# Hybrid block, start of the first projection: features 0 to 255 of x are multiplied without their shift, which is added later as a bias; x is scaled on VectorE and GpSimd

## The chip, the core and the metric

The kernel runs on one core of a Trainium2 chip. The metric is the device time of one execution in microseconds; the median of three runs is given. A core has TensorE (PE, with its weight loads as PEld), VectorE (DVE), ScalarE (ACT), GpSimd (POOL) and SyncE (SP). Here SP issues the DMAs. Each engine has its own queue of instructions and works through it in order; semaphores order the engines among each other.

## What is computed

One transformer block on x of 1024 tokens by 1024 features, in float32. Of the reference only the first part matters here:

```
cond = jax.nn.silu(c)
mod = cond @ w_ada[l] + b_ada[l]
sh_a, sc_a, gt_a, sh_m, sc_m, gt_m = jnp.split(mod, N_MOD, axis=-1)
h = rms_norm(x, g_attn_pre[l]) * (1 + sc_a) + sh_a
proj = h @ w_in[l]
```

The projection is followed by rotary embedding, two kinds of attention, an output projection, a residual add, and an MLP with a squared ReLU (1024 to 4096 and back). w_ada is 1024 by 6144; its columns 0 to 1023 give the shift sh_a and columns 1024 to 2047 the scale sc_a.

## The kernel before

**Order of the work.** The instructions are put in order by a list scheduler in the kernel's own Python code (`Sched`, L178). Each step has a modelled duration, dependencies, resources that it takes and gives back (buffers, PSUM banks), and a priority. `pick` (L263) takes for each engine the step that can start first; the key is start time, then priority, then order of creation (`PW`, L151, is 0). A step can have alternatives on several engines; then the one that would end first is taken, with 1.5 us in favour of POOL (`BONUS`, L149). The order that comes out is fixed in the program; on the chip each engine follows it and waits where it must.

**Precision.** Products are made at float32 accuracy from two parts: a value is split into a rounded high part (hi) and the rest (lo), and each dense product is three matmuls, hi·hi, lo·hi and hi·lo (L920, L921, L923).

**First stage.** The eight blocks of 128 tokens of x are loaded (L533), squared and summed on ACT (L629), their reciprocal root is taken on POOL (L468, L470), the block is scaled on ACT or DVE (L634, L635), transposed on PE (L642) and copied from PSUM by ACT or DVE (L646) into xnT, which has features on the partitions: 8 chunks k of 128 features by 1024 tokens.

**Modulation.** w_ada's 2048 columns come in four groups g of 256 features. A group is four tiles of 512 KB (L521), each with the shift's and the scale's 256 columns for two of eight row blocks. DVE multiplies the columns by cond and adds them up (L664, L666: eight instructions of 128x512 a group); PE sums over the partitions with a column of ones (L675), DVE makes from it the gain g_a and the shift s_a (L681 to L683). Group g covers the chunks k = 2g and 2g + 1. For each chunk `mod_chunk` (L693) makes the hi part on ACT (L705), the full value over it in xnT on ACT (L702) and the lo part on DVE (L708). Chunks 0 and 1 are done in two halves of 512 tokens, the others in one piece of 1024.

**First unit.** w_in's columns are used in six units of 384. The first unit's products run chunk by chunk as the chunks become ready (`first_unit`, L942), into six PSUM accumulators: halves x = 0 and 1 of the tokens, three column blocks c. 24 products an accumulator, 144 in all. The order is: chunks 0 and 1 for x = 0, then for x = 1, then chunks 2 and 3, 4 and 5, and at the end 6 and 7, an accumulator at a time. While PE waits early on, `filler` (L930) lets it multiply a tile of ones (L937) into the bank of the fourth accumulator, until that one is used itself. At the end `evac` (L794) takes an accumulator out of PSUM: rotary embedding on DVE, splitting into hi and lo, DMAs into the tiles of attention.

**Weights.** w_in's tiles come in through a ring of WS = 2 raw tiles, are rounded on ACT (L550), and the rest is taken on DVE (L555; for later units on DVE or POOL). `order0` (L482) is the order of the first loads on SP; the loads are issued in that order (`in_turn`, L501), each when its buffer is free.

**After the first unit** the other five units' projections (`proj_tile`, L974) stand beside the attention on PE; `prefer` (L2217) takes a dense product first while the projections lead the attention by less than LEAD = 0.8 of a unit. Output projection and MLP follow.

Of the kernel before, what the change touches and what calls it, by code (L numbers as in the profile page):

```python
# [177 lines left out]
class Sched:  # L178
# [57 lines left out]
    def spare(self, o):  # L236

        return self.slack if 15 <= o.prio < 25 else 2.5 if o.kind == "w" else 0.0
# [119 lines left out]
def hybrid_block(ctx: ExitStack, tc: tile.TileContext, x, positions, w_ada, b_ada, g_attn_post, w_in, w_out,  # L358
# [33 lines left out]
    WR, WS, NP, NV, NK, NQ, NT, NO = 6, 2, 4, 3, 2, 2, 2, 2  # L392
# [154 lines left out]
    def split_w(*a):  # L547
# [10 lines left out]
        if a[0] == 0:  # L558
            w_e[a] = op("DVE", t_dv(512), lo(V), [e], gives=[(r_wst, 1)], prio=3)
# [23 lines left out]
    e = op("ACT", 0.1, lambda: A.activation(cond[:], c_raw, AF.Exp, scale=-1.0), [e_c], prio=0)  # L583
# [6 lines left out]
    warm = p0.tile([P, KC], F32, name="warm")  # L590
# [35 lines left out]
    def x_block(tb):  # L626
        def f_sq():
# [5 lines left out]
        e = op(("ACT", "DVE"), (t_sb(D) + AP_COST, t_d2(D) + AP_DV),  # L633
               (lambda: A.mul(x_t[tb][:], x_t[tb][:], rstd[:, tb:tb + 1]),  # L634
                lambda: V.tensor_scalar(x_t[tb][:], x_t[tb][:], rstd[:, tb:tb + 1], None, ALU.mult)), [e], prio=2)  # L635
# [16 lines left out]

    def mod_group(g):

        b = {}
# [30 lines left out]
        for half in ((0, 1) if g == 0 else (None,)):  # L686
# [6 lines left out]
    def mod_chunk(k, eg, half):  # L693
# [6 lines left out]
        def full(eng):  # L700
            if eng is A:
                return lambda: A.activation(h, h, AF.Identity, bias=s_a[:, k:k + 1], scale=g_a[:, k:k + 1])  # L702
            return lambda: V.tensor_scalar(h, h, g_a[:, k:k + 1], s_a[:, k:k + 1], ALU.mult, ALU.add)

        eh = op("ACT", t_sb(n) + 2 * AP_COST, lambda: A.activation(hh, h, AF.Identity, bias=s_a[:, k:k + 1],  # L705
                                                                  scale=g_a[:, k:k + 1]), deps, prio=0)
        e = op("ACT", t_sb(n) + 2 * AP_COST, full(A), [eh], prio=0)
# [21 lines left out]
    e_turned = op("POOL", 1.8, f_turned, [e_rope] + e_rs, prio=0)  # L729
# [7 lines left out]
    def tables_a():  # L737
        e_tab0 = op("POOL", 1.9, lambda: init_tabs(slice(0, 1024)), [e_c, e_turned], prio=0)
# [203 lines left out]
    def first_unit():  # L942
# [6 lines left out]
        for i, (k, part, x, c) in enumerate(order):  # L949
# [10 lines left out]
            def after(k=k, part=part):  # L960
                if part:
                    tick()
                if k == KC - 1:
                    sc.filler = None
            d = dense(0.454 if part == 0 else 0.227, emit,
                      [w_e[0, w_at(0, c, k)[0]], (e_hl if part else e_hh)[k, x]] + (e_xn[0] + e_xn[1] if a == 5 else []),
                      takes=[(r, 1)] if first else [], after=after, gives=[(r_w, 1)] if last[w_at(0, c, k)[0]] == i else [])
            if k == KC - 1 and part:
                yield (0, x, c, lambda a=a: accs[a], d, r)

    for a in first_unit():
        evac(*a)

    def proj_tile(u, x, c):  # L974
        b = []
        for k in range(KC):
# [9 lines left out]
            d = dense(0.681, emit, [w_e[u, w_at(u, c, k)[0]]], takes=[(r_pj, 1)] if k == 0 else [], gives=gives, after=tick)  # L986
# [28 lines left out]
    def open_attention():  # L1015
        if any(x.t is None for x in e_tab[0] + e_tab[1] + list(e_hl.values())):
# [1198 lines left out]
    LEAD = 0.8  # L2215
# [27 lines left out]
```

## Time and profile before

| | us |
|---|---|
| median of three runs | 1117.04 |
| lowest and highest | 1116.61, 1117.36 |
| the profiled execution | 1117.15 |
| its span, first to last instruction | 1114.9 |
| busy in the span: PE, DVE, ACT, POOL | 1100.7, 819.5, 630.3, 247.9 |

The granted clock of TensorE is 1.00 throughout the stretches shown below. A profile comes from one execution, and its span leaves out what lies before the first and behind the last instruction. A matmul's end is modelled and matmuls overlap, so that the pitch of their starts tells more than their durations. A row of the timeline gives start, duration, engine, line, operation, output and inputs, shapes and count, and in brackets the idle time before it and what ended it. A row of a group gives busy time, mean duration in ns, and idle time before its instructions.

### The profile page before, as it was taken

How to read it: one execution, taken by the hardware profiler on the slowest of the kernel's cores; microseconds unless marked ns; L12 is line 12 of the kernel's file. 1: busy time of each engine (PE TensorE's matmuls, PEld its weight loads, DVE VectorE, ACT ScalarE, POOL GpSimd, SP SyncE). 2: the span in 40 equal slices, each digit the busy share in tenths (PEclk: the TensorE clock that was granted, in tenths of full speed). 3: DMA queues.
4: the chain of work that ended last, by engine and by line, in shares of the span. 5: the costliest groups of instructions: out<-in, count | busy, mean ns of one | idle time of the engine just before them, and what ended most of it. 6: DMA issues, size and time to landing. Idle time of an engine off the chain costs nothing.

```text
span 1114.9 us, 15568 instructions
## 1 busy us (share of the span) xinstructions
PE 1100.7 (99%) x5393; PEld 917.0 (82%) x5393; DVE 819.5 (74%) x1388; ACT 630.3 (57%) x1092; POOL 247.9 (22%) x316
## 2 busy tenths in 40 slices
PE   8999999999999999999999999999999999999996
PEld 7788888888888888888888888888888888888885
DVE  7877777666777666689798654798643996537998
ACT  8768776464656666577674335643154632347542
POOL 2158768666742231110000000000000000000003
PEclk9999999999999999999999999999999999999999
DMA  9756676454513734656751369521578013584104
GB/s 350 227 180 192 195 261 198 146 207 159 186 43 140 263 103 131 227 211 243 276 217 38 109 240 334 175 76 39 201 267 308 26 57 113 189 320 152 39 20 151
DMA packets 94110, 195.39 MB, mean 175 GB/s; under 512 B 9008, under 2 KB 31664, under 8 KB 94032
## 3 DMA queue, kind: packets, MB, share of 16 engines
q1 hardware_dynamic: 94032, 194.40, 50.3%
q8 instruction: 43, 0.70, 0.3%
q14 instruction: 35, 0.29, 0.1%
HBM read 141.80 MB, written 33.03 MB: 157 GB/s over the span
## 4 chain that ended last, share of the span: by engine, by line
PE 85%; DVE 7%; DMA 3%; issue 2%; ACT 1%; SPq 0%; POOL 0%; POOLq 0%; DVEq 0%; ACTq 0%
PE mlp_ps L2057 17%; PE mlp_ps L2055 17%; PE mlp_ps L2056 17%; PE pj L920 5%; PE pj L923 5%; PE pj L921 4%; PE s_ps L1203 3%; PE y_ps L1609 2%; PE y_ps L1611 2%; PE y_ps L1610 2%; PE o_ps L1338 2%; DMA wa<-in_w_ada 2%; PE pt_ps L1308 1%; PE s_ps L1258 1%; PE o_ps L1350 1%
## 5 line engine op out<-in xcount | busy, mean ns | idle before, releaser
L2055 PE MATMUL mlp_ps<-hw 128*128 128x512 f32 x896 | 348.9, 389 | 0.2 <-DVE u L2092 0.2
L2057 PE MATMUL mlp_ps<-hw 128*128 128x512 f32 x896 | 348.6, 389 | 0.0
L2056 PE MATMUL mlp_ps<-hw 128*128 128x512 f32 x896 | 348.6, 389 | 0.0
L2055 PEld LDWEIGHTS mlp_ps<-hw 128*128 128x128 f32 x896 | 168.2, 188 | 35.5 <-DVE u L2092 0.6
L2056 PEld LDWEIGHTS mlp_ps<-hw 128*128 128x128 f32 x896 | 168.2, 188 | 35.1
L2057 PEld LDWEIGHTS mlp_ps<-hw 128*128 128x128 f32 x896 | 168.2, 188 | 34.7
L1819 DVE TENSOR_TENSOR hw<-w,hw 128x1024 fp32r<-128x1024 f32 x96 | 114.6, 1221 | 98.1 <-ACT hw L1812 97.9
L1812 ACT CAST hw<-w 128x1024 fp32r<-128x1024 f32 x96 | 97.7, 1048 | 127.5 <-PE mlp_ps L2057 86.8
L2165 POOL TENSOR_TENSOR st<-st,nhalf 128x1 f32<-128x1 f32 x8 | 8.0, 1010 | 591.8 <-DVE st L2163 591.8
L920 PE MATMUL pj<-hw,w_hl 128*128 128x512 f32 x240 | 102.3, 426 | 0.0
L923 PE MATMUL pj<-hw,w_hl 128*128 128x512 f32 x240 | 94.6, 394 | 0.0
L921 PE MATMUL pj<-hw,w_hl 128*128 128x512 f32 x240 | 94.3, 393 | 0.0
L1326 DVE TENSOR_TENSOR ph<-pt_ps,ph 128x512 fp32r<-128x512 f32 (+1 forms) x110 | 69.1, 647 | 31.4 <-ACT ph L1322 31.0
L1812 ACT CAST hw<-u 128x1024 fp32r<-128x1024 f32 x48 | 48.6, 1051 | 63.2 <-PE mlp_ps L2057 63.2
L1322 ACT CAST ph<-pt_ps 128x512 fp32r<-128x512 f32 (+1 forms) x110 | 58.4, 556 | 31.5 <-PE pt_ps L1311 25.2
L1819 DVE TENSOR_TENSOR hw<-u,hw 128x1024 fp32r<-128x1024 f32 x48 | 56.9, 1218 | 17.8 <-ACT hw L1812 17.8
L1229 ACT ACTIVATE p_sb<-p_sb,mn 128x128 f32<-128x128 f32 (+3 forms) x64 | 49.7, 777 | 33.6 <-DVE mn L1222 32.9
L1234 POOL TENSOR_SCALAR p_sb<-p_sb,den 128x128 f32<-128x128 f32 (+3 forms) x64 | 49.8, 783 | 75.6 <-DVE den L1232 69.6
L2113 DVE TENSOR_TENSOR yacc<-yacc,mlp_ps 128x512 f32<-128x512 f32 x96 | 62.0, 681 | 3.3 <-PE mlp_ps L2057 3.3
L1070 POOL TENSOR_TENSOR ada_acc<-ada_acc,wa_st 128x512 f32<-128x512 f32 x42 | 55.6, 1323 | 3.5
L923 PEld LDWEIGHTS pj<-hw,w_hl 128*128 128x128 f32 x240 | 45.1, 188 | 10.4
L1609 PE MATMUL y_ps<-hw,oh 128*128 128x512 f32 x128 | 52.1, 407 | 0.0
(215 smaller groups left out, 1971.0 us busy)
## 6 DMA issues: line engine op xcount, KB each, us to landing
hw<-s_dram SPq DMA_DIRECT2D x84, 512.0 KB, 4.3
wa_st<-in_w_ada SPq DMA_DIRECT2D x32, 512.0 KB, 5.2
w<-in_w_up SPq DMA_DIRECT2D x32, 512.0 KB, 5.6
w<-in_w_down SPq DMA_DIRECT2D x32, 512.0 KB, 6.7
s_dram<-hw SPq DMA_DIRECT2D x28, 512.0 KB, 3.8
qt<-hl SPq DMA_DIRECT2D x40, 256.0 KB, 2.6
w_st<-in_w_in SPq DMA_DIRECT2D x36, 256.0 KB, 3.0
x_sb<-in_x SPq DMA_DIRECT2D x16, 512.0 KB, 5.5
```

The source lines that it names most:

```text
L920: T.matmul(ps, w[:, 0, n], h[0], start=(k == 0), stop=False)
L921: T.matmul(ps, w[:, 1, n], h[0], start=False, stop=False)
L923: T.matmul(ps, w[:, 0, n], h[1], start=False, stop=(k == KC - 1))
L1322: A.copy(b["ph"][:, 0, :w], b["pt"][:, :w])
L1326: V.tensor_tensor(b["ph"][:, 1, :w], b["pt"][:, :w], b["ph"][:, 0, :w].bitcast(F32), ALU.subtract)
L1609: T.matmul(ps[:], b["oh"][:, k], wh[:, c0:c0 + 512], start=(k == 4 * m), stop=False)
L1812: A.copy(out[j][0], flat(src[j]))
L1819: V.tensor_tensor(out[j][1], flat(src[j]), out[j][0].bitcast(F32), ALU.subtract)
L2055: T.matmul(ps[m][:], sh, mh, start=starts and k == 0, stop=False, **kw)
L2056: T.matmul(ps[m][:], sh, ml_, start=False, stop=False, **kw)
L2057: T.matmul(ps[m][:], sl, mh, start=False, stop=k == 3, **kw)
L2113: e = op("DVE", t_dv(512), lambda: V.tensor_tensor(y(), y(), ps[m][:], ALU.add), [e, ml.e_y[tb, n]], gives=gives, prio=1)
```

## The change

- **Group 0 in two parts.** Group 0's tiles (`LATE = (0,)`) hold only one kind of column: two tiles of 512 KB with the scale's 256 columns for all rows are loaded early, two with the shift's at the very end, as (10, 0) and (10, 1). `late_sums` adds up either kind in eight DVE instructions of 128x256.
- **Chunks 0 and 1 without shift.** Their hi part is x times gain on ACT, their lo part x times gain minus hi, in one DVE instruction; the pass over xnT falls away for them. The first unit multiplies these parts.
- **The shift as a bias.** When the shift's sums are there, it is split into hi and lo and multiplied by w_in's rows of chunks 0 and 1 (`f_b`, twelve matmuls of 128x2); the result is `bias0`, and ACT adds it to each of the first unit's six accumulators before they are taken out.
- **hw with the shift.** For the other units `mod_chunk(..., again=True)` makes chunks 0 and 1 once more, with the shift, after the first unit's last use of them; the other units' products wait for it (`e_rest`).
- **Scaling of x.** Blocks 0, 3 and 5 are scaled on DVE, blocks 1, 2, 4, 6 and 7 on POOL; before, ACT or DVE.
- **Other places.** The full pass of the other chunks may run on ACT or POOL; the first unit's lo weights on DVE or POOL; WS is 3; the loads' order is another; while `filler` is in force the scheduler's key counts priority with 0.03; the tables' steps on POOL have a lower priority; one activation with Exp is put ahead of cond's; the allowance for weight loads is 1.5 instead of 2.5; LEAD is 1.0. The weights' ring slots of chunks 0 and 1 are held until the bias products are done (`w_used`). The filler's own code stays as it is.

```diff
-        return self.slack if 15 <= o.prio < 25 else 2.5 if o.kind == "w" else 0.0
+        return self.slack if 15 <= o.prio < 25 else 1.5 if o.kind == "w" else 0.0
...
-            key = (s + PW * o.prio if e != "SP" else s, o.prio, o.seq)
+            key = (s + (0.03 if self.filler else PW) * o.prio if e != "SP" else s, o.prio, o.seq)
...
-    WR, WS, NP, NV, NK, NQ, NT, NO = 6, 2, 4, 3, 2, 2, 2, 2
+    WR, WS, NP, NV, NK, NQ, NT, NO = 6, 3, 4, 3, 2, 2, 2, 2
...
-    order0 = [("x", 0), ("x", 1), ("x", 2), (0, 0), (0, 1), ("x", 3), (0, 2), ("w", 0), (0, 3), ("w", 1)]
-    order0 += [("x", t) for t in range(4, TB)]
-    for g in range(1, 4):
-        order0 += [(g, 0), (g, 1), (g, 2), (g, 3)] + [("w", 2), ("w", 3), ("w", 4), ("w", 5)][(0, 0, 1, 3)[g]:(0, 1, 3, 4)[g]]
+    LATE = (0,)
+    order0 = [('x', 0), ('x', 1), ('x', 2), ('w', 0), ('x', 3), (0, 0), (0, 1), ('w', 1), ('x', 4), ('x', 5), (1, 0), ('x', 6), ('x', 7), (1, 1), (1, 2), ('w', 2), (1, 3), (2, 0), (2, 1), (2, 2), (2, 3), ('w', 3), (3, 0), ('w', 4), (3, 1), ('w', 5), (3, 2), (3, 3), (10, 0), (10, 1)]
...
+            if g % 10 in LATE:
+                c0 = (D if g < 10 else 0) + g % 10 * GW
+                nc.sync.dma_start(wa_t[g, j][:].rearrange("p (r n) -> p r n", r=4), ada_view[:, 4 * j:4 * j + 4, c0:c0 + GW])
+                return
...
-            w_e[a] = op("DVE", t_dv(512), lo(V), [e], gives=[(r_wst, 1)], prio=3)
+            w_e[a] = op(("DVE", "POOL"), (t_dv(512), t_ptt(512) + 1.5), (lo(V), lo(G)), [e], gives=[(r_wst, 1)], prio=3)
...
+        if 'DPPDPDPP'[tb] == "D":
+            e = op("DVE", t_d2(D) + AP_DV,
+                   lambda: V.tensor_scalar(x_t[tb][:], x_t[tb][:], rstd[:, tb:tb + 1], None, ALU.mult), [e], prio=1)
+        else:
+            e = op("POOL", t_pts(D),
+                   lambda: G.tensor_scalar(x_t[tb][:], x_t[tb][:], rstd[:, tb:tb + 1], 1.0, ALU.mult, ALU.mult), [e], prio=1)
...
+    def late_sums(a, i):
...
+                    if j == r == 0:
+                        b["acc"] = p0.tile([P, 512], F32, name="acc_a", tag="acc_a", bufs=2)
+                        V.tensor_scalar(b["acc"][:, :GW], w, cj, None, ALU.mult)
+                    else:
+                        V.scalar_tensor_tensor(b["acc"][:, :GW], w, cj, b["acc"][:, :GW], ALU.mult, ALU.add)
...
+            for k in range(2):
+                T.matmul(b["ps"][:, k:k + 1], b["acc"][:, k * P:k * P + P], ones[:, 0:1], start=True, stop=True)
...
+        if k // 2 in LATE and not again:
+            eh = op("ACT", t_sb(n) + AP_COST, lambda: A.mul(hh, h, g_a[:, k:k + 1]), deps, prio=0)
+            e = op("DVE", t_dv(n) + AP_DV, lambda: V.scalar_tensor_tensor(
+                hl, h, g_a[:, k:k + 1], hh.bitcast(F32), ALU.mult, ALU.subtract), [eh], prio=0)
...
+        if again:
+            eh = op("ACT", t_sb(n) + 2 * AP_COST, lambda: A.activation(hh, h, AF.Identity, bias=s_a[:, k:k + 1],
+                                                                      scale=g_a[:, k:k + 1]), [eg] + e_used[k], prio=6)
+            e = op(("ACT", "DVE"), (t_sb(n) + 2 * AP_COST, t_d2(n) + 2 * AP_DV), (full(A), full(V)), [eh], prio=4)
+            e_rest[k] = op("DVE", t_dv(n), lambda: V.tensor_tensor(hl, h, hh.bitcast(F32), ALU.subtract), [e], prio=4)
+            return
...
-        e = op("ACT", t_sb(n) + 2 * AP_COST, full(A), [eh], prio=0)
+        e = op(("ACT", "POOL"), (t_sb(n) + 2 * AP_COST, t_pts(n) + 0.6), (full(A), full(G)), [eh], prio=0)
...
+                    def shift(a=a, c=c):
+                        A.activation(accs[a][:], accs[a][:], AF.Identity, bias=bias0[:, c:c + 1])
+                    d = op("ACT", t_ps(512) + AP_COST, shift, [d, e_bias], prio=2)
...
+            for c in range(3):
+                for k, part in jobs:
+                    i, n = w_at(0, c, k)
+                    T.matmul(b_ps[0][:, c], w_hl[0, i][:, part, n * P:n * P + P], s_hl[:, k],
+                             start=(k, part) == jobs[0], stop=(k, part) == jobs[-1])
...
-            d = dense(0.681, emit, [w_e[u, w_at(u, c, k)[0]]], takes=[(r_pj, 1)] if k == 0 else [], gives=gives, after=tick)
+            d = dense(0.681, emit, [w_e[u, w_at(u, c, k)[0]]] + ([e_rest[k]] if k in e_rest else []), takes=[(r_pj, 1)] if k == 0 else [], gives=gives, after=tick)
...
-    LEAD = 0.8
+    LEAD = 1.0
```

More of the change, by code (lines that the diff above doesn't have):

```diff
@@ L582, in hybrid_block @@
     e_init = op("DVE", 0.4, f_init, prio=0)
-    e = op("ACT", 0.1, lambda: A.activation(cond[:], c_raw, AF.Exp, scale=-1.0), [e_c], prio=0)
+    warm = p0.tile([P, KC], F32, name="warm")
+    e = op("ACT", 1.5, lambda: A.activation(warm[:], nhalf[:], AF.Exp), [e_init], prio=0)
+    e = op("ACT", 0.1, lambda: A.activation(cond[:], c_raw, AF.Exp, scale=-1.0), [e_c, e], prio=0)
     def f_cond():
@@ L964, in after @@
                     sc.filler = None
+                if last[w] == i:
+                    w_used(w)
             d = dense(0.454 if part == 0 else 0.227, emit,
                       [w_e[0, w_at(0, c, k)[0]], (e_hl if part else e_hh)[k, x]] + (e_xn[0] + e_xn[1] if a == 5 else []),
-                      takes=[(r, 1)] if first else [], after=after, gives=[(r_w, 1)] if last[w_at(0, c, k)[0]] == i else [])
+                      takes=[(r, 1)] if first else [], after=after)
+            if c == 2 and part:
+                e_used.setdefault(k, []).append(d)
```

85 lines of the change are left out of this document (74 added, 11 removed).

## The prediction

> **What bounds the kernel now.** I read the page first, its busy times and its chain; then busy time by stretches of the span; then the chain in order of time; then single instructions of the first 67 us.
>
> ```profile
> PE 1100.7 (99%) x5393; PEld 917.0 (82%) x5393; DVE 819.5 (74%) x1388; ACT 630.3 (57%) x1092; POOL 247.9 (22%) x316
> PE 85%; DVE 7%; DMA 3%; issue 2%; ACT 1%; SPq 0%; POOL 0%; POOLq 0%; DVEq 0%; ACTq 0%
> ```
>
> PE is busy 99% of the span, but busy is not useful: matmuls on a tile of ones (L937) count too. The stretches tell the stages apart (busy us and count of PE, PEld, DVE, ACT, POOL; then clock, DMA share, GB/s):
>
> ```profile
> core 0: us, PE busy (x) PEld busy (x) DVE busy (x) ACT busy (x) POOL busy (x), PEclk, DMA share, GB/s
> 9.70:22.90 13.20, 11.71 (x73) 9.09 (x73) 10.16 (x21) 12.26 (x22) 3.86 (x8) 1.00 1.06 402
> 22.90:34.40 11.50, 11.23 (x71) 9.21 (x69) 11.23 (x17) 9.86 (x17) 6.60 (x11) 1.00 0.95 331
> 34.40:39.70 5.30, 4.77 (x21) 3.31 (x21) 5.20 (x11) 4.82 (x8) 0.00 (x0) 1.00 0.71 213
> 39.70:50.20 10.50, 10.50 (x52) 8.82 (x51) 10.29 (x18) 7.56 (x7) 0.00 (x0) 1.00 0.76 214
> 50.20:66.60 16.40, 16.40 (x79) 13.47 (x78) 11.02 (x17) 11.20 (x16) 6.00 (x5) 1.00 0.35 115
> 66.60:330.00 263.40, 262.82 (x1505) 223.90 (x1504) 192.51 (x522) 172.66 (x420) 183.06 (x230) 1.00 0.56 181
> 330.00:520.00 190.00, 188.67 (x993) 157.65 (x994) 138.95 (x283) 125.15 (x215) 35.96 (x45) 1.00 0.51 178
> ```
>
> From 39.7 us on PE has no hole: 26.9 of 26.9 us up to the end of the first unit, then 262.82 of 263.40 and 188.67 of 190.00. So later stages can win at most 0.6 + 1.3 us, and what the first unit wins or loses reaches the end nearly whole. Up to 34.4 us the picture is another one:
>
> ```profile
> L937 PE MATMUL acc<-ones_r 128*128 128x512 f32 x61 | 19.5, 445 | 1.5 <-DVE nhalf L580 1.5
> ...
> 34.46 0.19 PEld L920 LDWEIGHTS acc<-hw,w_hl 128*128 128x128 f32 x1
> ...
> 66.64 0.19 PEld L920 LDWEIGHTS pj<-hw,w_hl 128*128 128x128 f32 x1
> ```
>
> The first row groups PE's matmuls on ones, the other two are from the timeline. 34.46 us is the first dense product on rows 512 to 1023 of x (x=1 in the code); 66.64 us is the first product of the second unit. Of the first unit's 144 products 18 (features 0 to 255, x=0) stand ahead of it in the code's order. The chain in order of time says what held it up:
>
> ```profile
> 27.30 3.52 DMA wa<-in_w_ada
> 30.82 1.55 DVE acc_a L666
> ...
> 36.39 0.61 DVE hw L708
> 37.05 0.96 PE acc L923 x3
> ...
> 46.45 2.72 PE acc L923 x12
> ```
>
> Loads of w_ada, DVE's weighted sums, then PE alone. Twelve products take 2.72 us, 0.227 us each. The 126 products after 34.46 need 28.6 of the 32.2 us to 66.64. DVE is as full as PE: 11.23 of 11.50, 5.20 of 5.30, 10.29 of 10.50 us. Two limits lie close together, and the forecast turns on which of them decides afterwards.
>
> **The change, step by step.** *The first half-1 product.* It needs all eight blocks of x.
>
> ```profile
> L533 SPq DMA_DIRECT2D x_sb<-in_x x8: 328/386/507, 1.6 to 13.9; - x8
> DMA to landing us min/median/max: 3.8/6.5/7.7
> 26.57 1.06 ACT L629 ACTIVATE junk<-x_sb 128x1024 bf16<-128x1024 f32 x1
> 28.18 0.92 POOL L470 TENSOR_TENSOR rstd<-rs_t,nhalf 128x1 f32<-128x1 f32 x1
> 29.14 1.16 ACT L634 ACTIVATE x_sb<-x_sb,rstd 128x1024 f32<-128x1024 f32 x1 [1.42 <-POOL rstd L470]
> 31.50 1.07 ACT L646 COPY xnT<-pxt 128x512 f32<-128x512 f32 x2 [0.23 <-PE pxt L642]
> 32.46 1.52 ACT L705 ACTIVATE hw<-xnT,s_a,g_a 128x512 fp32r<-128x512 f32 x2
> L702 ACT ACTIVATE xnT<-xnT,s_a,g_a 128x512 f32<-128x512 f32 x4 | 3.0, 805 | 0.0
> ```
>
> The last x block lands by 13.9 + 7.7 = 21.6 us, but its square starts at 26.57: 5 us in ACT's queue. After: three tiles of w_ada stand ahead of it instead of four, 0.52 MB at 402 GB/s, 1.3 us; it lands at 20.3. ACT loses the two 0.8 us L702 passes on these features and the scalings of x, so I let the square wait 1 us for one instruction in progress: 21.3. Square and rsqrt take 2.5 us (26.57 to 29.10 now), which gives 23.8; then the scaling, now on POOL:
>
> ```profile
> L1234 POOL TENSOR_SCALAR p_sb<-p_sb,den 128x1024 f32<-128x1024 f32 x8 | 9.5, 1183 | 8.1 <-DVE den L1232 6.9 <-PE pt_ps L1308 1.2
> ```
>
> 1.18 us by this row, the nearest, against ACT's 1.16, plus 0.5 for what POOL or DVE has in progress: scaled at 25.5 instead of 30.3. Transposes, eviction and the first L705 take 3.0 us (30.3 to 33.3): first product at 28.5 instead of 34.46, **6.0 us sooner**.
>
> *What PE has to do after it.* The same 126 products. Moved behind it, as they no longer fall into idle time: group 1's column sums and the table transposes.
>
> ```profile
> 32.23 1.03 PE L744 MATMUL ptab<-head,turned 128*64 128x128 f32 x8
> 33.57 0.95 PE L675 MATMUL pm<-ones,acc_a 128*128 128x1 f32 x8
> ```
>
> 0.95 and 0.9. New: the late shift's four column products, half of the second row, 0.45, and the twelve bias products of 128x2. No row shows one of these; the nearest are 128x1 at 0.12 and 128x512 at 0.227, so 1.4 to 2.7 in all; I take 1.4, as two columns are nearer to one. Sum 3.7. Won: between 34.46 and 39.7 PE does 18 products, 4.1 us, in 5.2; the lo half now comes straight from x and its scale, without waiting for L702, so I take 1.1 off. Net **2.6 us back**.
>
> *Other edits.* The shift of the first unit's six accumulators is an ACT pass of 128x512, about 0.6 us as L646 above; second-unit products cover it on PE, and if they didn't, it would cost 0.6 once. The rewriting of hw for features 0 to 255 (two L705, two L702, two L708 of 128x1024, about 1.2 us each) and the late sums fall behind the last sums of group 3, where DVE idles 5.4 of 16.4 us (50.2 to 66.6); without that cover the second unit's first product waits for them, bounded by all of it on one queue, about 7 us. The warming of the activation table comes ahead of a load that ACT awaits anyway: nothing. The third slot for raw weights, LEAD 1.0 and the smaller allowance for weight loads rearrange stages where PE has 1.9 us of holes: gain between 0 and 1.9, loss not excluded; I take 0 and keep ±2 for the range. No wait is added ahead of a DMA that another queue needs before 50 us: the two late tiles are last in the load order.
>
> Sum: 6.0 − 2.6 = 3.4 us. The profiled execution took 1117.15 us (span 1114.9), 0.1 over the median of 1117.04: **1113.7 us**.
>
> **What speaks against it: DVE and POOL.** One row shows that they are not independent:
>
> ```profile
> L666 DVE SCALAR_TENSOR_TENSOR acc_a<-wa,cond,acc_a x28: 742/752/1544, 11.0 to 49.4; 128x512 f32<-128x512 f32 x28
> 30.82 2.33 DVE L666 SCALAR_TENSOR_TENSOR acc_a<-wa,cond,acc_a 128x512 f32<-128x512 f32 x2
> 30.79 1.03 POOL L733 COPY tab<-head 128x1024 f32<-128x1024 f32 x1
> ```
>
> The one sum of 1544 ns instead of 752 is the one at 30.82, and it ran while POOL copied 128x1024: a POOL instruction of 1.03 us cost DVE 0.79. The Trainium skill, "SBUF — State Buffer", section "Who interferes with whom", says that a DVE instruction with two SBUF inputs contends with a GpSimd one that reads SBUF, and that such a lock blocks the later one fully. This row agrees. By that rule alone, nine instructions of 1.18 us would cost DVE 10.6 us, 2.4 more than in the first rival below, which would end at 1121.6.
>
> **The rivals.** *Slower: POOL holds up DVE.* Until the last sums of group 3 the change gives POOL five scalings of x and probably four passes of L702's kind (features 256 to 767). No row shows POOL multiplying by one column and adding another; L1234 multiplies by one, the copy of 1.03 us bounds it below, twice L1234 above. So nine instructions of about 1.18 us, each worth 1.18 × 0.79/1.03 = 0.9 us of DVE while DVE adds without pause. That is 8.2, and about 0.8 for weight halves that go to POOL.
>
> ```profile
> L646 DVE COPY xnT<-pxt 128x512 f32<-128x512 f32 x4 | 2.8, 688 | 0.9 <-PE pxt L642 0.8
> L708 DVE TENSOR_TENSOR hw<-xnT,hw 128x1024 fp32r<-128x1024 f32 x6 | 7.1, 1219 | 2.4 <-ACT xnT L702 2.4
> L708 DVE TENSOR_TENSOR hw<-xnT,hw 128x512 fp32r<-128x512 f32 x4 | 2.6, 684 | 0.0
> ```
>
> On the other side DVE loses: half the elements of group 0's eight sums, (1219 − 684)/2 = 0.27 us each, 2.0; one scaling, 0.75; up to four evictions, 2.8, that an emptier ACT can take. Sum 5.5, and up to 1.5 of idle time before 22.9. Net +2.0 at the last sums. Behind them 1.05 are won (L702 need not follow two L705), PE's 1.9 of new products is lost, and 0.85 of slack before the lo halves is used: +2.0, **1119.2 us**. It decides from about seven blocked instructions of the nine on. For it: DVE's 98% from 22.9 to 50.2. Against it: POOL's scalings may meet evictions from PSUM or DVE's idle time before 22.9 (3.0 us).
>
> *No change.* Five or six of nine block; DVE's last sums come about as now, 1115 to 1119, midpoint **1117**.
>
> *More.* If neither ACT nor POOL queues the last block (1.5 us) and the tables and column sums find holes (1.8), 3.4 + 3.3 = 6.7: **1110.4 us**. For it: ACT has 1.6 us of idle from 22.9 to 34.4 even now. Against it: POOL runs three of the last four scalings in a row.
>
> **How the numbers follow.** Forecast 0.42, more 0.18, no change 0.20, slower 0.20. Within 0.2%, 2.2 us, is about what a measurement can tell from no change. Forecast and "more" lie below that: faster 0.60, same 0.20, slower 0.20. The range reaches from 1108.5 (the 1110.4 with the 1.9 of later holes) to 1119.2, the slower rival's own time; what lies beyond, half of that rival and a little of "more", is about 0.15. Forecast alone: 1111 to 1116.
>
> **What would show it.** First half-1 product at 28.5 us (27 to 30), the second unit's first at 63.3. If the first is early and the second is not, DVE or POOL decided: then sums longer than 1.2 us stand beside POOL's rows, and PE has holes between 40 and 65 us. Fewer matmuls on ones by some 20. A second-unit product waiting for L708 would mean that the rewriting has no cover; holes of PE over 2 us after 70 us would show that the rearranged stages lose. I am wrong altogether if the last block's square still waits 5 us on ACT, or if POOL's scaling takes over 2 us.

## The result and the profile after

The changed kernel takes **1132.86 us** in the median of four executions (1130.07 to 1135.11), the kernel before in the same session 1117.2: a ratio of 1.014, 95% interval 1.0115 to 1.0164. The forecast was 1113.7 with a range up to 1119.2; the loss of the medians is 15.7 us. The profiled execution, the fastest of the four, took 1130.07 us, 12.9 more than the profiled execution of before. The page's busy times and chain, and busy time by stretches (columns as before; the eighth number is the granted clock):

```profile
PE 1102.6 (98%) x5392; PEld 917.8 (81%) x5392; DVE 836.7 (74%) x1404; ACT 626.2 (56%) x1096; POOL 263.9 (23%) x317
...
PE 77%; DVE 13%; issue 4%; DMA 2%; ACT 2%; POOL 1%; SPq 0%; POOLq 0%; DVEq 0%; ACTq 0%
```

```profile
22.90:34.40 11.50, 9.50 (x62) 7.69 (x61) 9.48 (x12) 8.02 (x15) 10.88 (x16) 1.00 1.09 354
34.40:39.70 5.30, 5.30 (x20) 4.39 (x21) 5.16 (x10) 2.48 (x3) 1.41 (x2) 0.68 1.09 354
39.70:66.60 26.90, 22.86 (x104) 18.48 (x102) 26.10 (x37) 9.38 (x11) 11.81 (x8) 0.94 0.34 91
66.60:330.00 263.40, 259.86 (x1482) 221.15 (x1481) 195.84 (x515) 178.10 (x431) 178.30 (x215) 1.00 0.57 184
```

DVE's share of the chain has risen from 7% to 13%. From 39.7 to 66.6 us PE has lost 4 us that it did not lack before, while DVE is busy 26.1 of 26.9 us. The clock, 1.00 throughout before, is 0.68 and 0.94 in two stretches. PE's rows show where it stands still:

```profile
32.78 0.40 PE L982 MATMUL acc<-hw,w_hl 128*128 128x512 f32 x1
...
34.40 1.05 PE L722 MATMUL pm<-ones,acc_a 128*128 128x1 f32 x8 [0.99 <-DVE acc_a L713]
...
46.78 1.02 PE L722 MATMUL pm<-ones,acc_a 128*128 128x1 f32 x8 [1.90 <-DVE acc_a L713]
...
64.16 0.58 PE L677 MATMUL pm<-ones,acc_a 128*128 128x1 f32 x4 [2.14 <-DVE acc_a L670]
...
75.73 0.47 PE L982 MATMUL pj<-hw,w_hl 128*128 128x512 f32 x1 [0.61 <-DVE hl L882]
```

The first row is the first product on rows 512 to 1023, 1.9 us sooner than the matmul of before (34.70); the last is the second unit's first product, 8.9 us later (66.87). Between them PE waits three times for column products whose sums DVE has not finished. The products themselves could run; they stand behind in PE's queue. The chain in order of time is DVE's work over long stretches:

```profile
31.34 1.57 DVE acc_a L713
...
37.88 0.76 DVE acc_a L713
38.67 1.65 DVE acc_a L713
...
59.95 1.32 DVE acc_a L670
61.30 1.32 DVE acc_a L670
62.65 1.38 DVE acc_a L670
64.16 0.58 PE pm L677 x4
...
66.71 1.23 PE pb L1068 x12
```

A sum of 128x512 takes 0.76 us in one row and 1.65 in the next; a late sum of 128x256 takes 1.32 or more where 0.5 would do. Beside each long one POOL is at work. Two sums and differences of DVE, and POOL's rows at that time:

```profile
41.85 2.31 DVE L770 TENSOR_TENSOR hw<-xnT,hw 128x1024 fp32r<-128x1024 f32 x1
44.08 2.55 DVE L713 SCALAR_TENSOR_TENSOR acc_a<-wa,cond,acc_a 128x512 f32<-128x512 f32 x2
46.55 1.22 DVE L770 TENSOR_TENSOR hw<-xnT,hw 128x1024 fp32r<-128x1024 f32 x1
```

```profile
41.35 3.95 POOL L557 TENSOR_TENSOR w_hl<-w_st,w_hl 128x512 fp32r<-128x512 f32 x2
50.73 2.26 POOL L752 TENSOR_SCALAR xnT<-xnT,g_a,s_a 128x1024 f32<-128x1024 f32 x1 [5.43 <-ACT hw L767]
```

The same difference (L770) takes 2.31 us while POOL makes weight halves and 1.22 us when POOL rests. POOL is held up as well: 2.26 us for a pass whose shortest is 1.19. From the second unit to the end of the projections another 4.2 us are lost: the last product comes at 384.93 us instead of 371.87, so 8.9 us became 13.1, and what follows takes the same time in both (745.1 and 745.3 us to the end of the execution).

### The profile page after: what moved, and what is told of

Its sections match the earlier page's. It is cut to its first block, busy times and chain, and to the rows that moved or that the text cites. A ratio compares the mean times of both kernels' runs of the same rounds, so it can differ in the third digit from the quotient of the medians.

```text
span 1128.3 us, 15582 instructions
## 1 busy us (share of the span) xinstructions
PE 1102.6 (98%) x5392; PEld 917.8 (81%) x5392; DVE 836.7 (74%) x1404; ACT 626.2 (56%) x1096; POOL 263.9 (23%) x317
## 4 chain that ended last, share of the span: by engine, by line
PE 77%; DVE 13%; issue 4%; DMA 2%; ACT 2%; POOL 1%; SPq 0%; POOLq 0%; DVEq 0%; ACTq 0%
PE mlp_ps L2169 16%; PE mlp_ps L2171 16%; PE mlp_ps L2170 16%; PE pj L982 3%; PE pj L985 3%; PE pj L983 3%; PE s_ps L1317 3%; PE y_ps L1723 1%; PE y_ps L1725 1%; PE y_ps L1724 1%; PE o_ps L1452 1%; PE s_ps L1372 1%; PE pt_ps L1422 1%; PE pt_ps L1429 1%; PE o_ps L1464 1%
## 5 line engine op out<-in xcount | busy, mean ns | idle before, releaser
L1440 DVE TENSOR_TENSOR ph<-pt_ps,ph 128x512 fp32r<-128x512 f32 (+1 forms) x110 | 68.4, 646 | 33.1 <-ACT ph L1436 33.1
L1436 ACT CAST ph<-pt_ps 128x512 fp32r<-128x512 f32 (+1 forms) x110 | 58.1, 556 | 31.2 <-PE pt_ps L1425 27.7
```

What stands on the lines that cost most here:

```text
L1436: A.copy(b["ph"][:, 0, :w], b["pt"][:, :w])
L1440: V.tensor_tensor(b["ph"][:, 1, :w], b["pt"][:, :w], b["ph"][:, 0, :w].bitcast(F32), ALU.subtract)
```

## Experiments

All times by one table: median, ratio to the kernel before with its 95% interval, and from each run's trace, in us: the first product on rows 512 to 1023 (half 1), the second unit's first product, the last product of the projections, and the time at half clock in the profiled execution, between its first and last full clock. A stretch at half clock costs PE at most half its length.

| run | us | ratio | half 1 | unit 2 | last | half clock |
|---|---|---|---|---|---|---|
| before | 1117.2 to 1117.8 | | 34.70 | 66.87 | 371.9 | 0 |
| changed | 1132.86 | 1.014 (1.0115–1.0164) | 32.78 | 75.73 | 384.9 | 6.8 |
| a_nopool | 1126.61 | 1.0086 (1.0069–1.0103) | 31.73 | 73.55 | 381.1 | 3.4 |
| a_full_act | 1130.83 | 1.012 (1.0105–1.0135) | 33.54 | 75.57 | 384.4 | 6.8 |
| a_lead_old | 1137.57 | 1.0176 (1.0159–1.0193) | 34.21 | 82.13 | 391.0 | 17.1 |
| b_pool | 1126.79 | 1.0083 (1.0068–1.0098) | 39.73 | 74.47 | 380.2 | 3.4 |
| b_late | 1134.34 | 1.015 (1.0134–1.0165) | 33.06 | 75.57 | 389.6 | 17.1 |
| b_order | 1125.23 | 1.0065 (1.0048–1.0082) | 36.16 | 72.84 | 379.6 | 0 |
| b_lead | 1121.53 | 1.0036 (1.0023–1.0049) | 36.12 | 68.21 | 377.2 | 0 |
| a_notlate | 1130.81 | 1.0117 (1.0102–1.0132) | 39.08 | 76.01 | 384.9 | 6.8 |
| b_order_q | 1125.26 | 1.0068 (1.005–1.0086) | 34.39 | 73.28 | 380.0 | 6.8 |
| b_pool_q | 1130.05 | 1.011 (1.0094–1.0126) | 40.60 | 79.87 | 384.9 | 6.8 |
| b_late_q | 1129.75 | 1.0107 (1.0089–1.0126) | 33.99 | 67.04 | 383.2 | 10.2 |
| a_nopool_q | 1130.47 | 1.0114 (1.0098–1.013) | 31.86 | 72.82 | 385.1 | 10.2 |
| a_memset | 1117.67 | 1.0002 (0.9992–1.0011) | 30.30 | 63.88 | 371.0 | 0 |
| a_fill | 1129.35 | 1.0108 (1.0094–1.0121) | 33.41 | 75.92 | 384.3 | 3.4 |
| a_memset_fill | 1122.38 | 1.0044 (1.0028–1.0059) | 31.25 | 69.72 | 377.0 | 0 |
| b_leadonly | 1120.55 | 1.0027 (1.0017–1.0037) | 35.46 | 67.64 | 375.6 | 0 |
| a_dve | 1134.14 | 1.0145 (1.013–1.016) | 33.29 | 76.97 | 389.1 | 13.7 |
| a_dve_w | 1132.83 | 1.0145 (1.0117–1.0172) | 31.56 | 71.56 | 388.2 | 10.2 |

The names beginning with a_ start from the changed kernel, those with b_ from the kernel before.

### Parts of the change taken out, or put in alone

**POOL's shares taken out, all of them or the full passes alone:**

```diff
-        if 'DPPDPDPP'[tb] == "D":
...
+        e = op(("ACT", "DVE"), (t_sb(D) + AP_COST, t_d2(D) + AP_DV),
...
-        e = op(("ACT", "POOL"), (t_sb(n) + 2 * AP_COST, t_pts(n) + 0.6), (full(A), full(G)), [eh], prio=0)
+        e = op("ACT", t_sb(n) + 2 * AP_COST, full(A), [eh], prio=0)
...
-            w_e[a] = op(("DVE", "POOL"), (t_dv(512), t_ptt(512) + 1.5), (lo(V), lo(G)), [e], gives=[(r_wst, 1)], prio=3)
+            w_e[a] = op("DVE", t_dv(512), lo(V), [e], gives=[(r_wst, 1)], prio=3)
```

> The changed kernel, with the three kinds of work that it gives to POOL back where they were: scalings of x on ACT or DVE, the full passes of features 256 to 767 on ACT, the low weight halves of the first unit on DVE. Theory A (POOL stretches DVE's sums, and the sums set the end of the first unit): the nine sums and differences stretched to 1.3 to 2.3 us fall back to their usual length, about 8 us of DVE; ACT gets 7 passes back, so 5 to 8 us of the 15.7 us loss go: 1125 to 1128, and no sum over 1.2 us between 23 and 56 us except beside POOL's table copy. Rival B (the late sums for the shift and the second writing of hw are extra DVE work that sits in front of the first unit's last products): nothing of this goes, 1131 to 1134. Rival C (holes of PE halve its clock): falls only as far as holes fall.

> The changed kernel with only the full passes of features 256 to 767 (L752, 2.26 us each on POOL) back on ACT; scalings of x stay shared by DVE and POOL. Theory A: the stretched instructions after 36 us (1.64, 1.58, 2.31, 1.76, 1.49 us, about 4.5 us over their usual length) go: 1127 to 1129. Rival B: 1131 to 1134. If all of POOL's harm is in the scalings of x ahead of 34 us, no change either, and the run without any POOL share is faster than this one.

Without any share 6.3 us of 15.7 go, as theory A had it. Without the full passes alone theory A's 1127 to 1129 is missed: the 2.0 us are within the intervals. But the order of every engine is another in both, so the loss is not yet pinned to the stretching.

**The planner's three numbers, taken back in the changed kernel, and put alone into the one before:**

```diff
-    LEAD = 1.0
+    LEAD = 0.8
...
-    WR, WS, NP, NV, NK, NQ, NT, NO = 6, 3, 4, 3, 2, 2, 2, 2
+    WR, WS, NP, NV, NK, NQ, NT, NO = 6, 2, 4, 3, 2, 2, 2, 2
...
-        return self.slack if 15 <= o.prio < 25 else 1.5 if o.kind == "w" else 0.0
+        return self.slack if 15 <= o.prio < 25 else 2.5 if o.kind == "w" else 0.0
```

> The changed kernel with LEAD 0.8, two slots for raw weights and the old 2.5 us allowance for weight loads. PE's extra holes after the first unit cost about 4 us in the profile (263.40 - 259.86 against 263.40 - 262.82 from 66.6 to 330, of which most lies ahead of 75.7, and 1.3 us from 330 to 520). If the rearranged stages are at fault: 1129 to 1130. If everything follows from the late end of the first unit (theories A and B): 1131 to 1134.

> The kernel before with only LEAD 1.0, three slots for raw weights and the allowance of 1.5 us. My forecast put 0 +- 2 on it: 1115 to 1119. Undone in the changed kernel, these three cost 4.7 us, so a gain here, 1113 to 1115, would say that they help by themselves; no change, that they only help a kernel with a late first unit.

Neither theory had it: taken back they cost 4.7 us more, put in alone they cost 4.0. An edit's price is not its own here; it is that of the order that the scheduler makes around it. With the three numbers taken back the profiled execution is at half clock for 17.1 us instead of 6.8, which could make up to 5.1 us of difference.

**POOL's shares alone, the deferral alone, the load order alone, all but the deferral.** The edits are the parts of the change shown above.

> The kernel before with only POOL's shares added: five scalings of x on POOL, full passes and low weight halves of the first unit with POOL as an alternative. Nothing of the late shift, the load order or the fillers. Theory A: DVE's sums are stretched as in the changed kernel, so 4 to 8 us slower than before: 1121 to 1125. Rival B: POOL only relieves ACT, 1116 to 1118.

> The kernel before with only the shift deferred: the two half tiles of w_ada for the shift of features 0 to 255 last in its own load order, late sums, bias products, shifts of the accumulators, and the second writing of hw. No work of the first unit is given to POOL beyond what it had; old load order, LEAD, slots and allowance. Theory B (the deferred shift is itself a loss of the size that remains without POOL's shares, 9.4 us): 1123 to 1128, the late sums standing ahead of the low halves of features 768 to 1023 on DVE, and PE waiting for the late column products. If the deferral works as I forecast it and only POOL's shares and the load order harm: 1111 to 1116.

> The kernel before with only the changed kernel's load order (whole tiles of group 0, all four by the fifteenth load, as the shift isn't deferred). If the order is what remains without POOL's shares: 1121 to 1127. If the deferred shift is: 1115 to 1119.

> The changed kernel without the deferral (group 0 summed whole, from tiles in the same places of the load order), POOL's shares and all else left. If POOL's loss (9.4 us alone in the kernel before) and the deferral's (up to 9.4 in the changed kernel without POOL's shares) don't add up, because both are DVE's time in the same packed stretch: 1124 to 1128. If the deferral costs nothing by itself: 1130 to 1134. If the deferral is the larger loss and the load order softens POOL's: below 1122.

Each part alone loses: 9.4, 16.8 and 7.7 us, the first two more than any range given for them. Together with b_lead's 4.0 that is 38, far over the 15.7 of the whole; the parts do not add up. b_late is at half clock for 17.1 us, up to 8.5 of its 16.8. All but the deferral, a_notlate, is where its expectation put it if the deferral costs nothing by itself in the changed kernel. In b_pool, b_late and b_order a second thing had changed: no load of a tile was issued for 10 us or more, with the ten DMAs of the rotary tables standing on SP's queue ahead of group 3's tiles.

### The same with SP's queue mended

The ten table DMAs are issued behind w_ada's last tile:

```diff
-            load_ada(a, n)
+            load_ada(a, n); behind = gone[0]
...
-        e = load(f_rows_a, 655360, e_rows + [e_tab0], prio=-13, n=10)
+        e = load(f_rows_a, 655360, e_rows + [e_tab0, behind], prio=-13, n=10)
```

> The kernel before with the changed load order (as b_order), and one thing more: the ten DMAs of the rotary tables (L757 in the kernel before) are issued on SP's queue only behind the last tile of w_ada. PE, DVE and ACT get the same instructions in the same order as in b_order; only SP's order differs. Theory Q (in b_order the ten table DMAs, which wait for rows that ACT copies at 38.7 us, stand on SP ahead of group 3's last tiles, so that no load is issued from 31.45 to 46.6 us, and the order itself is harmless): 1116 to 1119. Rival (the order itself costs 7.7 us): 1123 to 1126.

> The kernel before with POOL's shares (as b_pool) and the table DMAs behind the last tile of w_ada on SP. In b_pool loads stood still from 34.19 to 44.37 us behind them. Theory A (POOL stretches DVE, and that is the loss): 1121 to 1125, as little of the 9.4 us is SP's. Theory Q (SP's order made most of the 9.4 us): 1116 to 1119.

> The kernel before with the deferral alone (as b_late) and the table DMAs behind the last tile of w_ada on SP. In b_late they held the loads from 27.69 to 40.07 us. Theory B (the deferral itself loses: late sums and second writing of hw in DVE's queue, column and bias products in PE's): 1122 to 1127. Theory Q (the deferral gains what I forecast once SP's queue is free): 1111 to 1116.

> The changed kernel without POOL's shares (as a_nopool) and with the table DMAs behind the last tile of w_ada on SP; the changed kernel itself has them there already, so this is the fair measure of what POOL's shares cost in it. If A and Q are all (POOL's shares are the loss of the changed kernel, and a_nopool only met SP's order instead): 1112 to 1118. If the deferral loses as well (theory B): 1120 to 1125.

Theory Q fell in all four runs; b_pool_q, at 1130.05, is above theory A's range too. With the table DMAs out of the way b_order_q keeps its whole loss. Its SP and DVE rows show the loads:

```profile
30.56 1.03 SPq L518 DMA_DIRECT2D wa<-in_w_ada  x2
44.90 0.34 SPq L538 DMA_DIRECT2D w_st<-in_w_in  x1
```

```profile
41.54 2.35 DVE L705 TENSOR_TENSOR hw<-xnT,hw 128x1024 fp32r<-128x1024 f32 x2
...
44.15 1.28 DVE L552 TENSOR_TENSOR w_hl<-w_st,w_hl 128x512 fp32r<-128x512 f32 x2
```

The loads stop all the same, from 31.2 to 44.9 us: the next one in turn is a weight tile, which needs one of two slots, and it is issued 0.75 us after DVE starts the low half that frees a slot. The table DMAs only filled a gap. Whether the changed kernel's third slot would cure this order alone was not tried. a_nopool_q has three slots, and its loads stop from 31.4 to 45.4 us as well, SP waiting 13.6 us for a low half on DVE. It misses both its forecasts and is 3.9 us slower than a_nopool. In both, DVE's sums are back at 782 ns in the mean: the stretch is gone, and another loss stands in its place. That the stopped loads are that loss was not tested, so neither run prices POOL's shares.

b_late_q shows the deferral without POOL's shares and without table DMAs ahead of the loads (which still stop from 28.5 to 36.7 us): its first unit ends as before, at 67.04, and it too misses both its forecasts. Then PE's rows run as follows, with one stretch below them:

```profile
70.25 0.48 PE L954 MATMUL pv<-head,vt 64*128 64x64 f32 x4 [2.37 <-ACT vt L948]
...
74.18 0.79 PE L986 MATMUL pj<-hw,w_hl 128*128 128x512 f32 x1 [2.30 <-DVE hw L766]
```

```profile
66.60:140.00 73.40, 67.49 (x357) 54.02 (x356) 56.48 (x157) 51.66 (x144) 53.71 (x84) 0.95 0.67 200
```

The second unit waits for the second writing of hw (L766) and for evictions that queue with it, and from 70.6 us on 6.8 us at half clock follow. In this stretch PE is busy 67.49 us instead of 72.88 before. From the second unit's first product to the last one of the projections pass 316.2 us instead of 305.0. In the changed kernel this loss is not seen, as there the second unit starts 8.7 us later.

### Every order kept, POOL's reads taken away

This kernel leaves out the values of the tiles that POOL would compute.

```diff
-                   lambda: G.tensor_scalar(x_t[tb][:], x_t[tb][:], rstd[:, tb:tb + 1], 1.0, ALU.mult, ALU.mult), [e], prio=1)
+                   lambda: G.memset(x_t[tb][:], 0.0), [e], prio=1)
...
-            return lambda: eng.tensor_scalar(h, h, g_a[:, k:k + 1], s_a[:, k:k + 1], ALU.mult, ALU.add)
+            return (lambda: G.memset(h, 0.0)) if eng is G else lambda: eng.tensor_scalar(h, h, g_a[:, k:k + 1], s_a[:, k:k + 1], ALU.mult, ALU.add)
...
+                G.memset(w[:, 1].bitcast(F32), 0.0) if eng is G and a[0] < 2 else eng.tensor_tensor(w[:, 1], w_raw[a][:], w[:, 0].bitcast(F32), ALU.subtract)
...
+        G.memset(tabs[0][:, cs], 1.0) if n == 1024 else G.tensor_copy(tabs[0][:, cs], scl[0].to_broadcast([P, n]))
```

> The changed kernel with every instruction on every engine in the same order; only what POOL does in the first unit is another thing: its scalings of x (L641), its full passes (L752), its low weight halves of the first two units (L557) and its copy into the table (L795) are memsets of the same tiles, so the values of those tiles are left out. A memset of 128x1024 takes POOL 0.95 us in these traces and DVE's sums beside one keep their 0.75. Theory A (POOL's reads from SBUF stretch DVE's instructions that read two operands from SBUF, by 12.7 us before the second unit's first product, and that is the loss of the first unit): stretch under 2 us, second unit's first product at 66 to 70 us instead of 75.7, time 1120 to 1126. Rival (the order of the queues and POOL's own lateness are the loss, the stretched sums only stand beside it): first product after 72 us, 1128 to 1133.

**15.2 us go**, more than theory A had, and the second unit's first product comes at 63.88 us. The groups of DVE up to that product, first of the changed kernel, then of this one (count | busy us, mean ns | idle before):

```profile
L713 DVE SCALAR_TENSOR_TENSOR acc_a<-wa,cond,acc_a 128x512 f32<-128x512 f32 x21 | 21.4, 1020 | 0.5
L670 DVE SCALAR_TENSOR_TENSOR acc_a<-wa,cond,acc_a 128x256 f32<-128x256 f32 x14 | 10.2, 729 | 0.4
L770 DVE TENSOR_TENSOR hw<-xnT,hw 128x1024 fp32r<-128x1024 f32 x6 | 8.4, 1399 | 0.0
...
L752 DVE TENSOR_SCALAR xnT<-xnT,g_a,s_a 128x1024 f32<-128x1024 f32 x2 | 2.6, 1292 | 0.0
L557 DVE TENSOR_TENSOR w_hl<-w_st,w_hl 128x512 fp32r<-128x512 f32 x3 | 2.5, 845 | 0.2 <-ACT w_hl L552 0.2
```

```profile
L713 DVE SCALAR_TENSOR_TENSOR acc_a<-wa,cond,acc_a 128x512 f32<-128x512 f32 x21 | 15.7, 749 | 0.5
L770 DVE TENSOR_TENSOR hw<-xnT,hw 128x1024 fp32r<-128x1024 f32 x6 | 7.3, 1216 | 0.0
L670 DVE SCALAR_TENSOR_TENSOR acc_a<-wa,cond,acc_a 128x256 f32<-128x256 f32 x14 | 6.8, 484 | 0.4
...
L557 DVE TENSOR_TENSOR w_hl<-w_st,w_hl 128x512 fp32r<-128x512 f32 x3 | 2.1, 685 | 0.2 <-ACT w_hl L552 0.2
L752 DVE TENSOR_SCALAR xnT<-xnT,g_a,s_a 128x1024 f32<-128x1024 f32 x2 | 1.6, 808 | 0.0
```

The counts are the same, only the means differ: 21 × 0.271 + 14 × 0.245 + 6 × 0.183 + 2 × 0.484 + 3 × 0.160 = 11.7 us, and PE's first product of the second unit moves by 75.73 − 63.88 = 11.9. That is the loss of the first unit and the better part of the whole. With the sums at their length PE's holes go, and with them the slow clock:

```profile
34.40:39.70 5.30, 5.30 (x27) 4.40 (x25) 5.19 (x7) 2.90 (x5) 2.85 (x4) 1.00 1.09 353
39.70:66.60 26.90, 26.82 (x132) 22.36 (x133) 25.90 (x47) 17.69 (x24) 6.70 (x8) 1.00 0.53 155
```

A memset is also a lighter load for POOL: 0.95 us stands in place of 1.12 to 1.19, 0.52 in place of 1.28, and it waits for less; from 22.9 to 34.4 us POOL is busy 7.71 us instead of 10.88. But DVE is what PE waits for, and a late POOL would show as idle time there. The same 118 instructions of DVE end ahead of the second unit's first product in both kernels, and DVE's idle time between them adds up to 8.59 us in the changed one and 8.57 here, while the instructions themselves take 70.8 and 58.7 us. So up to there the stretching is the loss, and POOL's lateness is not. Which instructions of DVE are hit is to be read in the changed kernel's later stages, where POOL works on. A difference that takes one operand from PSUM, then the sums L713 and DVE's weight halves, whose tensors all lie in SBUF, with minimum, median and maximum in ns:

```profile
L1440 DVE TENSOR_TENSOR ph<-pt_ps,ph x110: 537/680/694, 95.8 to 432.4; 128x512 fp32r<-128x512 f32 x78, 128x384 fp32r<-128x384 f32 x32
...
L713 DVE SCALAR_TENSOR_TENSOR acc_a<-wa,cond,acc_a x21: 743/752/1764, 23.0 to 54.3; 128x512 f32<-128x512 f32 x21
...
L557 DVE TENSOR_TENSOR w_hl<-w_st,w_hl x13: 674/693/1812, 12.0 to 320.0; 128x512 fp32r<-128x512 f32 x13
```

None of 110 is stretched, though 67 of them overlap a reading instruction of POOL by more than 0.1 us; the other two kinds reach more than twice their median.

### The clock

```diff
-            b["ps"] = px.tile([P, 2, 2], F32, name="pm", tag="x")
+            t = px.tile([P, 512], F32, name="pm", tag="x"); b["ps"] = t[:, 0:4].rearrange("p (k i) -> p k i", k=2)
+            [T.matmul(t[:], ones_r[:, :P], ones_r[:], start=True, stop=True) for _ in range((0, 5, 9, 0)[g])]
```

> The changed kernel with matmuls on ones ahead of three groups of column products, where PE waits for DVE: 5 ahead of group 1's, 9 ahead of group 2's, 9 ahead of the late shift's, 0.227 us each, into the bank that those column products use; nothing else. Theory C (holes of PE halve its clock for 3.41 us at a time, and each such window costs 1.7 us): no half clock between 35 and 53 us, second unit's first product 2 to 3.4 us sooner, 1128 to 1131 in the median. Rival (PE would only wait longer for DVE): within 1 us of the changed kernel, 1131.5 to 1134; matmuls that don't fit their hole would cost up to 1 us.

> Both edits together (values left out as with the memsets alone). If stretched sums make the holes and the holes the half clock, the fillers find little to do: within 2 us of the memsets alone, to either side, as 23 fillers cost up to 5 us of PE where holes are gone. If the clock is a loss of its own: 2 to 3.4 us less than the memsets alone.

The slow clock is seen in the pitch of PE's rows in the changed kernel, 0.43 us at first and 0.23 us later:

```profile
36.21 0.63 PE L982 MATMUL acc<-hw,w_hl 128*128 128x512 f32 x1
36.64 0.63 PE L983 MATMUL acc<-hw,w_hl 128*128 128x512 f32 x1
...
39.28 0.39 PE L983 MATMUL acc<-hw,w_hl 128*128 128x512 f32 x1
39.51 0.39 PE L982 MATMUL acc<-hw,w_hl 128*128 128x512 f32 x1
```

The Trainium skill, "TensorE: Matmul & The Clock Gate", section "Part 1: The HAM clock gate", says that the clock halves after an idle window of about 3.4 us and comes back after a busy one; the half clock of the changed kernel's trace lasts 3.41 us each of two times, after the holes at 33 to 34 and 45 to 47 us, so the trace agrees on the length. That a partly filled window is enough is this trace's: the longest hole is 2.1 us, and that one, ahead of 64.16, had no half clock behind it.

With fillers the clock is 1.00 from 34.4 to 39.7 us, and one window of 3.41 us at half clock is left, from 57.8. But the second unit's first product is no sooner (75.92): there DVE decides, and a faster PE only waits longer, as the rival had it. The median still falls by 3.5 us to 1129.35, into theory C's range and out of the rival's, while the intervals of the two ratios just overlap; the changed kernel's executions show mean clocks of 0.988 to 0.995 and these 0.996 to 0.999. So the fillers seem to prevent further slow windows that the profiled execution did not have; where those lie no trace here shows. They may also be why the median lost 15.7 us and the profiled execution 12.9. Where no holes are (a_memset_fill) the 23 fillers cost 4.7 us, their full 23 × 0.227 = 5.2 but for half a microsecond, and more than the 2 us expected.

### LEAD alone, and two versions that keep all values

The kernel before with `LEAD = 1.0`:

> The kernel before with LEAD 1.0 alone. With the three slots and the allowance of 1.5 it lost 4.0 us, 1.3 of them ahead of the second unit. If LEAD makes the later loss: 1119.5 to 1121.5, the loss between the second unit's first product and the last product of the projections. If the slots and the allowance make it: 1117 to 1118.5.

2.9 of b_lead's 4.0 us are LEAD's. From the second unit's first product to the last product of the projections pass 308.0 us instead of 305.0.

```diff
-        if 'DPPDPDPP'[tb] == "D":
+        if 'DPPDDDDD'[tb] == "D":
...
-        e = op(("ACT", "POOL"), (t_sb(n) + 2 * AP_COST, t_pts(n) + 0.6), (full(A), full(G)), [eh], prio=0)
+        e = op(("ACT", "DVE"), (t_sb(n) + 2 * AP_COST, t_d2(n) + 2 * AP_DV), (full(A), full(V)), [eh], prio=0)
...
-            w_e[a] = op(("DVE", "POOL"), (t_dv(512), t_ptt(512) + 1.5), (lo(V), lo(G)), [e], gives=[(r_wst, 1)], prio=3)
+            w_e[a] = op("DVE", t_dv(512), lo(V), [e], gives=[(r_wst, 1)], prio=3)
```

a_dve has these edits and the table DMAs behind w_ada's last tile; a_dve_w also has the low halves of the second unit's weights on DVE.

> The changed kernel with POOL's reads taken to engines that can do them without stretching a sum: from the fourth block on x is scaled by DVE (one operand from SBUF, 0.74 us each), the full passes go to ACT or DVE, the low weight halves of the first unit to DVE, and the table DMAs stay behind w_ada's last tile. DVE gets at most 3 scalings, some full passes of 0.81 and 2 halves of 0.68, 4 to 6 us of work, and is rid of 12.7 us of stretch less what the halves of the second unit's weights still stretch (some 2 us). By theory A: second unit's first product at 67 to 71 us, 1119 to 1124. If the full DVE queue loses as much as the stretch did: 1126 to 1131.

> The same, and the low halves of the second unit's weights on DVE too, so that POOL has the table copy alone to do beside the sums of the first unit after 30 us. Theory A: 0 to 2 us less than the run beside it, 1118 to 1123; more work for DVE in the second unit may take that back.

Both come out above every range given for them. Take each instruction of DVE ahead of the second unit's first product against the shortest of its kind: the stretch is down from 12.7 us in the changed kernel to 3.2 and 2.1, but the shortest times add up to 64.5 and 64.9 us instead of 57.8. In a_dve PE waits for DVE at the same place:

```profile
61.94 0.58 PE L677 MATMUL pm<-ones,acc_a 128*128 128x1 f32 x4 [3.90 <-DVE acc_a L670]
```

In a_dve_w it waits 3.19 us for DVE right ahead of the second unit. Both are at half clock for long (13.7 and 10.2 us). DVE had no room for what POOL had taken over. No version came out that beats the kernel before.

## Why the prediction was wrong

- **What bounds the kernel: right.** Two limits close together, PE and DVE, and the forecast turned on which decides. It was DVE: 26.10 of 26.90 us busy from 39.7 to 66.6 while PE lost 4. The sign named for it came: long sums beside POOL's rows, and holes of PE between 40 and 65 us.
- **First half-1 product at 28.5: wrong by 4.3 us** (32.78; 30.30 with the memsets). I let the last block's square wait one instruction of ACT, to 21.3. Three squares stand in a row on ACT behind chunk 0's and 1's high parts, which wait for the gain:

```profile
20.30 1.34 ACT L755 ACTIVATE hw<-xnT,g_a 128x512 fp32r<-128x512 f32 x2 [1.07 <-DVE g_a L684]
21.54 1.04 ACT L632 ACTIVATE junk<-x_sb 128x1024 bf16<-128x1024 f32 x1
...
24.81 1.06 ACT L632 ACTIVATE junk<-x_sb 128x1024 bf16<-128x1024 f32 x1
```

  The last block lands at 20.37, as forecast, but its square starts at 24.81: it waits 4.4 us, not 1, and so nearly the 5 that were to mean "wrong altogether". Square and reciprocal root then take 3.8 us instead of 2.5, as POOL scales the block before first. The scaling itself is as forecast (1.24 us against 1.18 and half a microsecond). Matmuls on ones fell by 13 (61 to 48), not by some 20.
- **2.6 us back on PE: the terms right, the assumption wrong.** From the first half-1 product to the second unit's first pass 42.95 us instead of 32.17: 10.8 back. With the memsets it is 33.58, 1.4 back; the twelve bias products take 1.23 us against 1.4. On PE's side four holes make 5.6 us of the 10.8, two windows at half clock up to 3.4, the new products 1.7. What failed is that the 126 products were taken to run without waiting for DVE, once the first could start.
- **The step that failed is the price of POOL against DVE**, which stood under the first rival and was kept out of the sum. The mechanism was the right one and had its row; two sizes were off. I counted nine reading instructions of POOL at 0.9 us, and with the weight halves 9.0 us; up to the second unit's first product POOL runs nineteen (five scalings, five full passes, eight weight halves, the table copy), and the stretch is 11.7 by the groups, about 0.6 for each. The price of one was set too high and the number of them far too low. And I set 5.5 us of relief and 1.5 of idle time against it; DVE's own rows up to that product did not get shorter (each taken at the shortest of its kind, 57.8 us against 56.7 before), as the late sums came into the same stretch ahead of the last low halves instead of behind them, where 5.4 us of idle time were to hide them. The Trainium skill, "SBUF — State Buffer", section "Who interferes with whom", says that two SBUF inputs on DVE contend with GpSimd instructions that read SBUF, not with those that only write it; that one SBUF input contends only in a mode that uses both ports; and that `tensor_scalar` can enter such a mode. The runs agree: the sums are stretched beside POOL's reads and not beside its memsets, and L1440, with one operand in PSUM, never is. A scaling by `tensor_scalar` with a single tensor from SBUF (L638, 0.74 us at the shortest) took 1.52 us beside a read and 1.23 beside a memset; no row shows in which mode it ran.
- **Other edits at 0 ± 2: wrong.** LEAD costs 2.9 us alone, with slots and allowance 4.0; the changed kernel loses 4.2 us between the second unit's start and the projections' last product. That the two are the same 4 us is likely but was not shown, as taking them back made the changed kernel slower. With the memsets it loses 2.1 there.
- **The rewriting of hw has cover: true for the wrong reason.** It is hidden in the changed kernel, whose first unit ends late; in b_late_q, which ends it in time, 11.2 us are lost where I gave 7 as the bound. The wait for hw itself is 2.3 of them; holes for evictions and half clock are the most of the rest, and how much of that is the rewriting's is open.
- **The clock was not foreseen.** The half clock stands behind holes that the forecast didn't have, and goes with them.

With POOL's reads away, the second unit's first product is at 63.88 us; the forecast had 63.3. So the first unit gets about the 3 us that it was forecast to get. In part that is luck: its first half-1 product is 1.8 us later than forecast, 1.2 us less is lost behind it, and the memsets are shorter than what they replace. 2 of the 3 us are lost again by the last product of the projections (370.99 instead of 371.87), and the median of the executions (1115.82 to 1121.20) is that of the kernel before. So the forecast gain would have failed to come without the stretching too.

## What to carry over

Before work is moved to an idle engine, look whether that engine reads from the memory that the full engine's instructions read: price every instruction that moves by what it adds to the other's rows, over its full count and not only those that come to mind. When parts of a change are tried alone in a kernel whose order a scheduler makes, each trial gets another order; an experiment that keeps every queue as it is and changes only what one engine does there tells far more.

## What was not expected of the hardware

- POOL's memsets of 128x1024 (0.95 us) left DVE's sums at 749 ns in the mean, its reads stretched them to 1020; its writes alone did not matter to the sums.
- The stretch goes both ways: a weight half of POOL, 1.28 us at the shortest, took 2.26 (at 68.65) beside a difference of DVE (L765) that kept its 1.22.
- Holes of 1.0 and 1.9 us on PE were followed by 3.41 us at half clock each; one of 2.1 us was not.
